# Laying a small first piece on 30 partitions instead of 120, and declaring implied waits away

## Chip, cores, metric

One core of one Trainium2 chip. The metric is the device time of one execution in microseconds (us), as the median of several; the kernel before takes 394.75 us (394.6 to 394.81, 6 runs). All runs quoted here are fast (none lies over 1.5% above the fastest of its kernel). Ratios are the mean time of one kernel's fast runs over that of the other's of the same rounds, so not quite the ratio of the medians that are quoted beside them.

## The reference

```python
batch, channels, length = 32, 256, 4096      # x: float32, 134.2 MB
p, kernel_size = 2.0, 4
window = np.abs(x[:, :, start:end]) ** p     # start = 4 * i, end = start + 4
result[:, :, i] = (np.mean(window, axis=-1)) ** (1.0 / p)   # 33.6 MB
```

Four neighbours are squared, averaged, and the root is taken: 134 MB in, 34 MB out, and very little arithmetic.

## The kernel before

The data is seen as one flat array. Most of it goes through three big x tiles (128 partitions x 13184 columns), loaded on the SyncE queue. ScalarE squares in place, VectorE sums groups of four into an o tile, ScalarE takes the root, and one store per group goes out on ScalarE's queue, the last four on SyncE's. What does not fit these sizes, 840 columns of 128 rows (430 KB), is a small piece of its own, handled first.

```python
    W, O_W = 13184, 6592
    X_SLOTS, O_SLOTS = 3, 2
    ODD = 840
    groups = [2] * 9 + [3, 1]
    late = {7, 8, 9, 10}                       # groups stored on SyncE's queue, at the end
    # ...
    def root(g, o, ends):
        nc.scalar.activation(out=o, in_=o, func=Act.Sqrt, scale=1.0 / k)
        if ends and g not in late:
            store(g, nc.scalar)
    # ...
    Q = 120
    odd = ODD * P // Q                         # 896 columns of 120 rows
    t = o_tiles[1][0:Q, 0:odd]
    nc.sync.dma_start(out=t, in_=xf[(total - ODD) * P:total * P].rearrange("(p w) -> p w", p=Q))
    ahead = 0
    while ahead < n and loads[ahead][0] < X_SLOTS:
        load(ahead)                            # three big loads queued behind it
        ahead += 1
    nc.scalar.activation(out=t, in_=t, func=Act.Square)
    o = o_tiles[1][0:Q, odd:odd + odd // k]
    nc.vector.tensor_reduce(out=o, in_=t.rearrange("p (n j) -> p n j", j=k), ...)
    nc.scalar.activation(out=o, in_=o, func=Act.Sqrt, scale=1.0 / k)
    nc.scalar.dma_start(out=of[...].rearrange("(p w) -> p w", p=Q), in_=o)
    pending = []
    done = 0
    for i in range(n):
        # load ahead; per chunk: Square, total_sum; then the root of the chunk before
        # ...
    for job in pending:
        root(*job[1:])
    for g in sorted(late):
        store(g, nc.sync)
```

Of the kernel before, what the change touches and what calls it, by code (L numbers as in the profile page):

```python
# [1 line left out]

# [4 lines left out]


@with_exitstack
def kernel(  # L10
    ctx: ExitStack,
    tc: tile.TileContext,
    x: bass.AP,
    p: float,
    kernel_size: int,
    out: bass.AP,
):








    nc = tc.nc

    assert float(p) == 2.0, "kernel specialized for p == 2"
    k = int(kernel_size)
    assert k == 4, "kernel specialized for kernel_size == 4"  # L30

    P = nc.NUM_PARTITIONS
    fp32 = mybir.dt.float32
    Act = mybir.ActivationFunctionType
    xf = x.rearrange("b c l -> (b c l)")
    of = out.rearrange("b c l -> (b c l)")
    total = xf.shape[0] // P

    W, O_W = 13184, 6592
    X_SLOTS, O_SLOTS = 3, 2  # L40
    slots = [[(W, [4416, 4384, 4384])]] * 18
    slots += [[(6592, [3296, 3296])] * 2, [(6592, [3296, 3296]), (4216, [2112, 2104])]]
    ODD = 840
    groups = [2] * 9 + [3, 1]
    late = {7, 8, 9, 10}
    in_x = {9: (2, 0), 10: (2, 4944)}
    FINE, ENDS, LAG = range(22), (), 1
    PAIRS = 16


    loads = [(s, sum(w for w, _ in slot[:j]), *slot[j]) for s, slot in enumerate(slots)
             for j in range(len(slot))]
    n = len(loads)
    assert sum(w for _, _, w, _ in loads) + ODD == total

    firsts = [sum(groups[:g]) for g in range(len(groups))]
    assert sum(groups) == n
    group_of = [g for g, count in enumerate(groups) for _ in range(count)]
    columns = [sum(w for _, _, w, _ in loads[firsts[g]:firsts[g] + groups[g]])
               for g in range(len(groups))]  # L60

    x_pool = ctx.enter_context(tc.tile_pool(name="x_pool", bufs=1))
    o_pool = ctx.enter_context(tc.tile_pool(name="o_pool", bufs=1))

    x_tiles = [x_pool.tile([P, W], fp32, name=f"xt{j}") for j in range(X_SLOTS)]
    o_tiles = [o_pool.tile([P, O_W], fp32, name=f"ot{j}") for j in range(O_SLOTS)]
    ctx.enter_context(tc.manual_schedule())

    def block(flat, g, div):
        at, width = sum(columns[:g]) * P // div, columns[g] * P // div  # L70
        return flat[at:at + width].rearrange("(p w) -> p w", p=P)

    xs = {}

    def load(i):
        s, at, w, _ = loads[i]
        v = x_tiles[s % X_SLOTS][:, at:at + w]
        g = group_of[i]
        src = sum(loads[j][2] for j in range(firsts[g], i))
        nc.sync.dma_start(out=v, in_=block(xf, g, 1)[:, src:src + w])  # L80
        xs[i] = v

    ots = {}

    def store(g, queue):
        queue.dma_start(out=block(of, g, k), in_=ots[g])  # L86

    def root(g, o, ends):
        nc.scalar.activation(out=o, in_=o, func=Act.Sqrt, scale=1.0 / k)  # L89
        if ends and g not in late:  # L90
            store(g, nc.scalar)

    def total_sum(o, v, i):
        add = mybir.AluOpType.add
        if i < PAIRS:
            nc.vector.tensor_reduce(  # L96
                out=o, in_=v.rearrange("p (n j) -> p n j", j=k),
                axis=mybir.AxisListType.X, op=add,
            )
            return  # L100

        q = v.rearrange("p (n j) -> p n j", j=k)
        front = v[:, 0:v.shape[1] // 2]
        h = front.rearrange("p (n j) -> p n j", j=2)
        nc.vector.tensor_tensor(out=h, in0=q[:, :, 0:2], in1=q[:, :, 2:4], op=add)  # L105
        nc.vector.tensor_tensor(out=o, in0=h[:, :, 0], in1=h[:, :, 1], op=add)  # L106


    Q = 120
    odd = ODD * P // Q  # L110
    t = o_tiles[1][0:Q, 0:odd]
    nc.sync.dma_start(out=t, in_=xf[(total - ODD) * P:total * P].rearrange("(p w) -> p w", p=Q))  # L112
    ahead = 0
    while ahead < n and loads[ahead][0] < X_SLOTS:
        load(ahead)
# [3 lines that stand above are left out]
    nc.vector.tensor_reduce(  # L119
        out=o, in_=t.rearrange("p (n j) -> p n j", j=k),  # L120
        axis=mybir.AxisListType.X, op=mybir.AluOpType.add,
    )
    nc.scalar.activation(out=o, in_=o, func=Act.Sqrt, scale=1.0 / k)  # L123
    nc.scalar.dma_start(
        out=of[(total - ODD) * P // k:total * P // k].rearrange("(p w) -> p w", p=Q), in_=o,
    )
    pending = []
    done = 0
    for i in range(n):
        s, _, w, chunks = loads[i]  # L130
        while ahead < n and loads[ahead][0] < s + X_SLOTS:
            load(ahead)
            ahead += 1
        g = group_of[i]
        if i == firsts[g]:
            t, first = (o_tiles[g % O_SLOTS], 0) if g not in in_x else (x_tiles[in_x[g][0]], in_x[g][1])
            ots[g] = t[:, first:first + columns[g] // k]
            summed = rooted = 0
        assert sum(chunks) == w
        c = 0  # L140
        for step in chunks:
            v = xs[i][:, c:c + step]
            nc.scalar.activation(out=v, in_=v, func=Act.Square)  # L143
            total_sum(ots[g][:, summed:summed + step // k], v, i)
            while pending and pending[0][0] <= done - LAG:
                root(*pending.pop(0)[1:])
            done += 1
            c += step
            summed += step // k
            ends = summed == columns[g] // k  # L150
            if ends or i in FINE or (i in ENDS and c == w):
                pending.append((done - 1, g, ots[g][:, rooted:summed], ends))
                rooted = summed
# [6 lines that stand above are left out]
# [1 line left out]
_INS = ['x', 'p', 'kernel_size']  # L161
_OUTS = [((32, 256, 1024), 'float32')]

_NUMBERS = {'p': 2.0, 'kernel_size': 4}


# [26 lines left out]
```

## Time and profile before

| | before |
|---|---|
| time, median | 394.75 us |
| profiled span | 392.8 us |
| VectorE / ScalarE busy | 69% / 74% |
| the two transfer queues, share of 16 engines | 85.2% + 14.0% |
| bytes moved, mean rate | 167.79 MB, 427 GB/s |

The prediction below shows the lines behind this table. One more view is the chain of waits by line; each share is the part of the span in which the chain ran through that line:

```profile
by line: DMA xt<-in_x_dram 62.4%; ACT xt L143 17.0%; DVE ot L96 8.4%; issue 3.6%; ACT ot L89 3.3%; ACT xt L89 1.2%; DVE xt L105 0.8%; DVE xt L106 0.4%; ACTq L86 0.3%; SPq L80 0.2%; SPq L112 0.1%; ACTq L89 0.0%
```

Loads of x lead. "issue" at 3.6%, 14 us, is time for which the chain saw no releaser; whether it could be saved by removing waits is one of the questions here.

### The profile page before, as it was taken

To read this page: it belongs to the slowest core of one execution; us is meant where nothing else is said; L and a number is where in the kernel's file an instruction comes from. 1 tells how busy PE (TensorE), PEld (TensorE's weight loads), DVE (VectorE), ACT (ScalarE), POOL (GpSimd) and SP (SyncE) were. 2 spreads that over 40 slices of the span, in tenths; PEclk is the share of its full clock that TensorE was granted. 3 is DMA by queue.
4 is the path that set the end of the run, shared out by engine and by line. 5 is a ranking of instruction groups with operands and counts; after the bars stand their busy time and mean duration, and the time that the engine had idled before them with its cause. 6 is when DMAs were issued, how large, how long until landed. Compare 5 with 4: busy or idle time off the path is not lost.

```text
span 392.8 us, 341 instructions
## 1 busy us (share of the span) xinstructions
DVE 271.8 (69%) x77; ACT 292.5 (74%) x128; POOL 0.2 (0%) x4
## 2 busy tenths in 40 slices
DVE  1059989594959495949594959495949494778781
ACT  3088987776776777677867786868586859899990
POOL 0000000000000000000000000000000000000000
DMA  9999999999999989999999999999999999999997
GB/s 361 420 429 446 446 446 384 430 470 430 389 432 473 430 387 435 467 430 422 432 435 430 427 435 427 430 435 459 459 404 430 459 438 430 395 430 432 429 432 315
DMA packets 5024, 167.79 MB, mean 427 GB/s; under 512 B 558, under 2 KB 678, under 8 KB 926
## 3 DMA queue, kind: packets, MB, share of 16 engines
q1 hardware_dynamic: 3879, 144.04, 85.2%
q10 hardware_dynamic: 1143, 23.73, 14.0%
q14 instruction: 2, 0.02, 0.0%
HBM read 134.22 MB, written 33.55 MB: 427 GB/s over the span
## 4 chain that ended last, share of the span: by engine, by line
DMA 62%; ACT 21%; DVE 10%; issue 4%; SPq 0%; ACTq 0%
DMA xt<-in_x_dram 62%; ACT xt L143 17%; DVE ot L96 8%; ACT ot L89 3%; ACT xt L89 1%; DVE xt L105 1%; DVE xt L106 0%; ACTq L86 0%; SPq L80 0%; SPq L112 0%; ACTq L89 0%
## 5 line engine op out<-in xcount | busy, mean ns | idle before, releaser
L143 ACT ACTIVATE xt<-xt 128x4384 f32<-128x4384 f32 (+4 forms) x62 | 229.6, 3705 | 85.1 <-DMA xt<-in_x_dram 81.9
L96 DVE TENSOR_REDUCE ot<-xt 128x1096 f32<-128x4384 f32 (+1 forms) x48 | 227.0, 4731 | 90.1 <-ACT xt L143 89.8
L89 ACT ACTIVATE ot<-ot 128x1096 f32<-128x1096 f32 (+1 forms) x54 | 59.8, 1107 | 1.8 <-DVE ot L96 1.1
L105 DVE TENSOR_TENSOR xt<-xt 128x1648 f32<-128x1648 f32 (+4 forms) x14 | 28.4, 2032 | 16.0 <-ACT xt L143 16.0
L89 ACT ACTIVATE xt<-xt 128x824 f32<-128x824 f32 (+2 forms) x8 | 6.5, 817 | 1.9 <-DVE xt L106 1.9
L106 DVE TENSOR_TENSOR ot<-xt 128x1096 f32<-128x1096 f32 (+1 forms) x6 | 7.8, 1303 | 0.2
L106 DVE TENSOR_TENSOR xt<-xt 128x824 f32<-128x824 f32 (+2 forms) x8 | 7.5, 939 | 0.3
L119 DVE TENSOR_REDUCE ot<-ot 120x224 f32<-120x896 f32 x1 | 1.1, 1086 | 5.7 <-ACT ot L117 5.7
L117 ACT ACTIVATE ot<-ot 120x896 f32<-120x896 f32 x1 | 0.9, 949 | 2.7 <-DMA ot<-in_x_dram 2.7
L117 ACT ACT_TABLE_LOAD x1 | 1.3, 1283 | 0.7 <-PEq L174 0.7
L123 ACT ACT_TABLE_LOAD x1 | 1.3, 1283 | 0.0
L123 ACT ACTIVATE ot<-ot 120x224 f32<-120x224 f32 x1 | 0.4, 389 | 0.0
L174 POOL MEMSET const-bfloat16-1.0<- 128x1 bf16 x1 | 0.1, 101 | 0.0
L174 POOL MEMSET const-uint8-127<- 128x1 uint8 x1 | 0.1, 101 | 0.0
L174 POOL MEMSET const-float32-0.0<- 128x1 f32 x1 | 0.1, 99 | 0.2 <-issue 0.2
L174 POOL MEMSET const-float32-1.0<- 128x1 f32 x1 | 0.1, 99 | 0.0
## 6 DMA issues: line engine op xcount, KB each, us to landing
xt<-in_x_dram SPq DMA_DIRECT2D x18, 6592.0 KB, 39.9
out_dram<-ot ACTq DMA_DIRECT2D x7, 3296.0 KB, 27.6
xt<-in_x_dram SPq DMA_DIRECT2D x3, 3296.0 KB, 29.4
out_dram<-ot SPq DMA_DIRECT2D x2, 3296.0 KB, 30.0
out_dram<-xt SPq DMA_DIRECT2D x1, 2472.0 KB, 10.4
xt<-in_x_dram SPq DMA_DIRECT2D x1, 2108.0 KB, 26.8
out_dram<-xt SPq DMA_DIRECT2D x1, 527.0 KB, 7.1
ot<-in_x_dram SPq DMA_DIRECT2D x1, 420.0 KB, 4.0
```

The source lines that it names most:

```text
L89: nc.scalar.activation(out=o, in_=o, func=Act.Sqrt, scale=1.0 / k)
L96: nc.vector.tensor_reduce(out=o, in_=v.rearrange("p (n j) -> p n j", j=k), axis=mybir.AxisListType.X, op=add,)
L105: nc.vector.tensor_tensor(out=h, in0=q[:, :, 0:2], in1=q[:, :, 2:4], op=add)
L106: nc.vector.tensor_tensor(out=o, in0=h[:, :, 0], in1=h[:, :, 1], op=add)
L117: nc.scalar.activation(out=t, in_=t, func=Act.Square)
L119: nc.vector.tensor_reduce(out=o, in_=t.rearrange("p (n j) -> p n j", j=k), axis=mybir.AxisListType.X, op=mybir.AluOpType.add,)
L123: nc.scalar.activation(out=o, in_=o, func=Act.Sqrt, scale=1.0 / k)
L143: nc.scalar.activation(out=v, in_=v, func=Act.Square)
L174: nc = _bacc.Bacc("TRN2", target_bir_lowering=False, num_devices=1)
```

## The change

The small piece gets two descriptors for each of 15 DMA engines instead of eight (a descriptor moves one row of a transfer, and the trace records each as one packet), and waits that, in the words of the code, follow from other waits are declared away. The diff, cut to its core (a list `by_act` of ScalarE's instructions, `sums` of VectorE's and `stores` of the stores are kept for it; `by_load` stays empty):

```diff
+    def follows(ins, before):
+        for b in before:
+            tc.declare_no_dep(ins.ins, b.ins, reason="follows from other waits")
     def root(g, o, ends):
-        nc.scalar.activation(out=o, in_=o, func=Act.Sqrt, scale=1.0 / k)
+        r = nc.scalar.activation(out=o, in_=o, func=Act.Sqrt, scale=1.0 / k)
+        follows(r, by_act[:-1] + list(stores.values()))
+        by_act.append(r)
     # total_sum: the same with follows(r, sums[:-1]) on each sum
-    Q = 120
+    Q = 30
     # main loop:
-            nc.scalar.activation(out=v, in_=v, func=Act.Square)
+            r = nc.scalar.activation(out=v, in_=v, func=Act.Square)
+            follows(r, by_act[:-1])
+            by_act.append(r)
```

## The prediction

> **What bounds the kernel now.** I read the page's shares first, then its slices and DMA lines, then the timeline of the two ends, because a kernel whose transfers never pause can only be shortened at its ends or by moving fewer or better packets.
>
> The page (engines, then the DMA row of the 40 slices, packets and queues):
> ```profile
> DVE 271.8 (69%) x77; ACT 292.5 (74%) x128; POOL 0.2 (0%) x4
> ...
> DMA  9999999999999989999999999999999999999997
> ...
> DMA packets 5024, 167.79 MB, mean 427 GB/s; under 512 B 558, under 2 KB 678, under 8 KB 926
> ## 3 DMA queue, kind: packets, MB, share of 16 engines
> q1 hardware_dynamic: 3879, 144.04, 85.2%
> q10 hardware_dynamic: 1143, 23.73, 14.0%
> ```
> No compute engine is above 74%, while the two transfer queues together fill 85.2 + 14.0 = 99.2% of 16 engines' span, and the row of slices has no hole before the last. The chain of waits puts most of its time (62.4%) on loads of the x tiles. So the bytes bound the kernel.
>
> Could the end still be a compute tail? ScalarE is 90% busy or more in the last slices. The stretches at the end (length, busy us with counts, clock, DMA share, GB/s) answer that:
> ```profile
> 360.00:376.00 16.00, 12.39 (x9) 16.00 (x9) 0.00 (x0) 1.00 1.00 427
> 376.00:386.00 10.00, 6.73 (x6) 6.84 (x7) 0.00 (x0) 1.00 0.99 425
> 386.00:393.00 7.00, 0.00 (x0) 0.00 (x0) 0.00 (x0) 1.00 0.62 261
> ```
> The last store is issued at 384.8 us (timeline of the SyncE queue, which ends with two stores from 380.26 on, 4.88 us in all), the engines run full until past 386, and still move 7 x 261 = 1.83 MB after 386. From 384.8 on that is 1.83 + 1.2 x 425/1000 = 2.3 MB, some 5.4 us of work at 427 GB/s, already queued or just issued; only 0.54 MB of it is the last store. ScalarE and VectorE could be some 3 to 4 us later in the tail without moving the end. The tail is bound by the queue of stores too.
>
> Last, the start, where the change acts (timeline: start, length, engine, line, operation, idle before and releaser):
> ```profile
> 0.73 0.46 SPq L112 DMA_DIRECT2D ot<-in_x_dram  x1
> 1.24 1.30 SPq L80 DMA_DIRECT2D xt<-in_x_dram  x3
> 4.74 0.95 ACT L117 ACTIVATE ot<-ot 120x896 f32<-120x896 f32 x1 [2.73 <-DMA ot<-in_x_dram]
> 5.71 1.28 ACT L123 ACT_TABLE_LOAD   x1
> 5.72 1.09 DVE L119 TENSOR_REDUCE ot<-ot 120x224 f32<-120x896 f32 x1 [5.72 <-ACT ot L117]
> 7.00 0.39 ACT L123 ACTIVATE ot<-ot 120x224 f32<-120x224 f32 x1
> 7.42 0.64 ACTq L124 DMA_DIRECT2D out_dram<-ot  x1
> 20.36 7.63 ACT L143 ACTIVATE xt<-xt 128x4416 f32<-128x4416 f32 x2 [12.97 <-DMA xt<-in_x_dram]
> ```
> The odd piece is done with compute at 7.4 us, and both engines then idle until the first big load lands at 20.36: 12.97 us of slack for it.
>
> I also read the trace's single DMA packets, one line of the tile each. They are very regular. A 52736 B row takes 1947 ns, a 26368 B one 978, the 896 B rows of the small store 41, the undisturbed 3584 B rows of the small load 140. The first packet starts at 1.75 us, the last ends at 391.42. All packet times add up to 389.72 us per engine; 1.75 + 389.72 = 391.47, so the engines have practically no idle time between, and 392.8 - 391.4 = 1.4 us of closing work follows. The time is therefore: start of the first packet + packet time of the slowest engine + 1.4, and on top the 1.9 us by which the measured 394.73 exceeds the profiled span, which the change does not touch.
>
> **What the Trainium skill says.** "DMA: Bandwidth & Descriptors", section "Where 436 GB/s comes from", gives 435.2 GB/s for the 16 ports. The trace agrees in size: 52736 B in 1947 ns is 27.1 GB/s per engine, 433 for 16, and the mean over the span is 427. The same page, "Why small descriptors are slow (HBM only)", names a fixed cost of about 3 cycles per packet. Here it is larger: taking 27.2 GB/s off each size leaves 1947 - 1939 = 8 ns, 978 - 969 = 9, 41 - 33 = 8, 140 - 132 = 8, some 7 cycles of its 850 MHz; the measurement decides. The same page, "Queues, rings and completion order", says that an engine goes round the queue rows packet by packet. The trace agrees: the 896 B packets of the small store come about 1.95 us apart on an engine, one after each 1947 ns row of x, which is why 105 KB take 20.7 us to land:
> ```profile
> ot<-in_x_dram SPq DMA_DIRECT2D x1, 420.0 KB, 4.0
> out_dram<-ot ACTq DMA_DIRECT2D x1, 105.0 KB, 20.7
> ```
> "SBUF — State Buffer", "Door 1: The DMA port swizzle", puts partitions 0 to 31 on 8 of the 16 ports. No run yet shows what that does here, but it is the one risk, below.
>
> **The change part by part.**
>
> *Descriptors.* The small load has 120 rows of 3584 B, the small store 120 of 896 B; afterwards both have 30, of 14336 and 3584 B. The bytes stay. That is 180 packets of 5024 fewer, 12 on each of 15 engines. At 8 ns each: 12 x 8 = 0.10 us off those engines. Checked by rows: load 8 x 140 = 1.12 against 2 x (14336/27.2 + 8 = 535) = 1.07; store 8 x 41 = 0.33 against 2 x 140 = 0.28. Sum -0.10 us, on the path, since the engines never idle. The sixteenth engine gains nothing, but it carries 35.8 KB less and is not last.
>
> *Contention at the start.* The 120 rows took 205 ns in the mean, not 140: 8 x 65 = 0.5 us of crowding per engine, and the first row of x on each engine took 2.15 to 2.54 us in place of 1.95, 0.35 more in the mean. First rows of x ended between 5.5 and 6.1 us. Crowding is thus already paid, some 0.85 us. Afterwards, 430 KB go to 8 ports: 430 KB / (8 x 27.2) = 1.98 us at best against 430 / (15 x 27.2) = 1.05. From 1.75 + some 0.2 for the first access the small load ends at about 3.9, the first row of x, then uncrowded, at 3.9 + 1.95 = 5.9. That lies inside the 5.5 to 6.1 of before. I choose +0.05 for this term, with -0.3 to +0.5 as likely.
>
> *Compute of the odd piece.* The rows get four times as long on a quarter of the lanes. Square: from the groups 128x3296 (2934 ns) and 128x4384 (3843 ns), 0.84 ns an element and 0.18 us fixed, so 3584 elements take 3.2 us, not 0.95. Reduction: 1086 ns at 896 elements and 4719 at 4384 give 1.04 per element, so 3.9, not 1.09. Root: some 0.93, not 0.39. Together 8.0 in place of 2.4, and the small store is issued at about 13 us instead of 7.4. All of that is inside the idle 12.97 us, so 0 on the path. With 2 packets an engine in place of 8, the store should land 6 to 8 us after issue, at about 20 in place of 28; the next writer of that tile comes at 55.5 us, so again 0. For the same reason the wait for this store moves from the first to the second sum of group 1 on VectorE without costing anything.
>
> *Waits.* The comparison of the instruction streams shows no change of order. ScalarE loses eight waits for stores and six waits for its own earlier instructions; VectorE loses one on itself. The store waits had been met before: VectorE had waited for the same store before writing what ScalarE then reads. The self-waits cost nothing visible: at 350.18 the square that carries one starts 0.09 us before the root ahead of it has ended (349.16 + 1.11), and the square at 76.03, with no such wait, also starts 0.09 before its root's end (75.02 + 1.10). Even 14 x 20 ns would vanish in ScalarE's idle time. 0 on the path.
>
> Sum: -0.10 + 0.05 + 0 + 0 = -0.05, say 394.73 - 0.1 = 394.6 after leaving the small chance that the start gets tidier.
>
> **The rivals.** First, the port jam: if the rows are dealt to engines in turn (engine e gets rows e and e+15), the first 15 rows lie on 4 ports, the next 15 on about 4 others, and the load needs 2 x 4 x 527 ns = 4.2 us instead of 2.1. Every engine would be some 2 us behind for good: 396.8. For it: the first rows on the 15 engines took from 138 to 668 ns, as if up to four shared something. Against: later rows ran at 140, with no sharing, and fair sharing should have stretched them all. I give a noticeable delay (over 0.7 us) one chance in seven. Second, the waits matter: a shorter ScalarE tail issues the last stores earlier. Against: 2.3 MB lie ahead of the engines when the last store is issued; even 1 us earlier would leave the end where it is. 394.7. Third, the small descriptors cost more than their own time, because each of the 8 store packets breaks into the stream of loads. Against: x rows beside them took 1947 ns, as elsewhere. If it were true, 0.3 us less: 394.3. Fourth, the slower odd piece delays something. It has 12.97 us of slack and needs 5.6: 394.7.
>
> **Range and chances.** The three runs before lie 0.2 us apart. The terms give -0.4 to +0.5, and the jam a tail to +2. So 394.6, with 394.0 to 395.6 for 8 in 10. A change of 2% would be 7.9 us; nothing in the sum reaches that in either direction: faster 0.005, same 0.985, slower 0.01.
>
> **What would show it.** Right: packets 4844 (5024 - 180), under 2 KB as many as under 512 B, under 8 KB 716; queue shares still 99%; small store issued near 13 us, landed within 8; first square of x between 20.1 and 20.9; the 14336 B packets taking near 1 us each instead of 535 ns, if 8 ports bind. Wrong: a first square later than 21.5 (the jam), the 14336 B packets at 535 (no port limit, then up to 0.5 us gained), holes in the DMA row, or an end that moved with the same start (then the waits or something later did it).

## The result and the profile after

394.65 us median (394.57 to 394.96, 6 runs) against 394.75 (394.6 to 394.81, 6 runs) before. The ratio is 0.9999, with a 95% interval of 0.9986 to 1.0012: the same. The interval is about half a microsecond wide to each side, so a gain of 0.1 us, as forecast, can't be told from none.

The page of the kernel after (engines, packets, queues):

```profile
DVE 274.6 (70%) x77; ACT 295.3 (75%) x128; POOL 0.2 (0%) x4
...
DMA packets 4844, 167.79 MB, mean 427 GB/s; under 512 B 558, under 2 KB 558, under 8 KB 716
...
q1 hardware_dynamic: 3789, 144.04, 85.2%
q10 hardware_dynamic: 1053, 23.73, 14.0%
```

180 packets are gone, exactly as counted; the bytes, the rate and the share of both queues have not moved. Both compute engines work 2.8 us more, for the longer rows of the small piece. Where those lie is in the timeline of its start:

```profile
0.73 0.45 SPq L131 DMA_DIRECT2D ot<-in_x_dram  x1
1.24 1.30 SPq L81 DMA_DIRECT2D xt<-in_x_dram  x3
4.75 3.19 ACT L136 ACTIVATE ot<-ot 30x3584 f32<-30x3584 f32 x1 [2.74 <-DMA ot<-in_x_dram]
7.96 1.28 ACT L142 ACT_TABLE_LOAD   x1
7.97 3.87 DVE L138 TENSOR_REDUCE ot<-ot 30x896 f32<-30x3584 f32 x1 [7.97 <-ACT ot L136]
11.88 0.95 ACT L142 ACTIVATE ot<-ot 30x896 f32<-30x896 f32 x1 [2.64 <-DVE ot L138]
12.86 0.63 ACTq L143 DMA_DIRECT2D out_dram<-ot  x1
20.48 7.63 ACT L162 ACTIVATE xt<-xt 128x4416 f32<-128x4416 f32 x2 [7.66 <-DMA xt<-in_x_dram]
```

The small store is issued at 12.86 us instead of 7.42, but ScalarE still waits for the first big load, 7.66 us instead of 12.97. The first square starts at 20.48 instead of 20.36. The list of transfers shows the one large local gain:

```profile
ot<-in_x_dram SPq DMA_DIRECT2D x1, 420.0 KB, 4.0
out_dram<-ot ACTq DMA_DIRECT2D x1, 105.0 KB, 7.8
```

The small store lands 7.8 us after its issue instead of 20.7, because an engine passes one packet of it between two rows of x, and there are now two in place of eight. Nobody was waiting for it. The end, in the same stretches as before:

```profile
376.00:386.00 10.00, 6.73 (x6) 6.86 (x7) 0.00 (x0) 1.00 0.98 424
386.00:393.00 7.00, 0.00 (x0) 0.00 (x0) 0.00 (x0) 1.00 0.63 266
```

Within two per cent the same end. Last, the chain of waits by line:

```profile
by line: DMA xt<-in_x_dram 62.5%; ACT xt L162 20.4%; DVE ot L110 8.4%; ACT ot L101 3.2%; ACT xt L101 1.2%; DVE xt L121 0.8%; DVE xt L123 0.4%; ACTq L98 0.3%; issue 0.3%; SPq L81 0.2%; SPq L131 0.1%
```

This looks like a success, and is not one: "issue" fell from 3.6% to 0.3%, 13 us, with the time unchanged. The squares' share rose by 3.4%. With the extra wait gone, the profile's bookkeeping follows the chain through the square instead of losing it: at 57 us the chain before has 3.72 us of "issue", the chain after a square of 3.86 us. A share of the chain is a label on time, not time that can be had.

### The profile page after: what moved, and what is told of

Same layout as the page of the kernel before. It is cut to its first block, busy times and chain, and to the rows that moved or that the text cites. A ratio compares the mean times of both kernels' runs of the same rounds, so it can differ in the third digit from the quotient of the medians.

```text
span 392.9 us, 329 instructions
## 1 busy us (share of the span) xinstructions
DVE 274.6 (70%) x77; ACT 295.3 (75%) x128; POOL 0.2 (0%) x4
## 2 busy tenths in 40 slices
DMA packets 4844, 167.79 MB, mean 427 GB/s; under 512 B 558, under 2 KB 558, under 8 KB 716
## 4 chain that ended last, share of the span: by engine, by line
DMA 63%; ACT 25%; DVE 10%; SPq 0%; ACTq 0%; issue 0%
DMA xt<-in_x_dram 63%; ACT xt L162 20%; DVE ot L110 8%; ACT ot L101 3%; ACT xt L101 1%; DVE xt L121 1%; DVE xt L123 0%; ACTq L98 0%; SPq L81 0%; SPq L131 0%
## 5 line engine op out<-in xcount | busy, mean ns | idle before, releaser
L138 DVE TENSOR_REDUCE ot<-ot 30x896 f32<-30x3584 f32 x1 | 3.9, 3874 | 8.0 <-ACT ot L136 8.0
L136 ACT ACTIVATE ot<-ot 30x3584 f32<-30x3584 f32 x1 | 3.2, 3189 | 2.7 <-DMA ot<-in_x_dram 2.7
L142 ACT ACTIVATE ot<-ot 30x896 f32<-30x896 f32 x1 | 0.9, 948 | 2.6 <-DVE ot L138 2.6
```

## The experiments

Ten kernels ran, all correct. The single packets quoted are from the records of the trace, a row of a tile each. These records do not name the engine, so a figure "per engine" is a sum over all packets divided by 16.

**1. Only the layout** (`Q = 30` in the kernel before).

> Only the rows are changed (30 instead of 120), no wait is taken away. Theory (the transfers are the bound and never pause; the change has two small terms of opposite sign in the start): the same time as the changed kernel, ratio to before 0.9985 to 1.001; mean packet time of the small load near 850 ns as in the changed kernel; first square of x near 20.5 us. Rival 'small packets break the stream of loads': 0.3 us or more faster than before, ratio 0.999 or less, and the gain is here, not in the other half of the change.

394.69 us (394.52 to 394.70, 5 runs) against 394.70 (394.57 to 395.08, 9 runs); ratio 0.9997, interval 0.9984 to 1.0009. The same, as the theory said. The small load's rows took 922 ns in the mean, and the first square started at 20.64 us. The stated rival, small packets breaking the stream of loads, is not seen: a gain of 0.3 us should have shown in the medians, which are 0.01 apart, though the interval alone would not exclude it. The trace of the kernel before speaks against it as well: the 120 packets of the small store pass between 11.3 and 25.7 us, and none of the 176 rows of x that start between 7 and 28 us took longer than 1956 ns, against the usual 1947.

**2. Only the waits** (the changed kernel with `Q = 120`).

> Only the waits are declared away, the rows stay 120. Theory: no change, ratio 0.9990 to 1.0010, 15 instructions or so fewer in the trace, same starts in the tail within 0.1 us. Rival 'the waits cost something': 0.2 us or more faster, with the last store issued earlier than 384.8 us and the end following it.

394.61 us (394.60 to 394.80, 5 runs) against 394.70; ratio 0.9997, interval 0.9984 to 1.0010. Again the same. The trace has 330 instructions, 11 fewer than before (not the 15 expected), though the waits in it are 15 fewer, as the prediction lists them. The two last stores begin at 380.19 us instead of 380.26; the squares that lost a self-wait start as before, for instance at 350.16 here and 350.18 there. The chain's "issue" share already falls to 0.2% here, so nearly all of it belongs to the waits and was worth nothing. (It is 2.7% in experiment 1, where no wait was declared away: the label moves by itself too.)

**3. The small piece on all 128 rows.**

```diff
-    Q = 120
+    Q = 128
```

> The small piece on 128 rows, 8 on each of 16 engines, no wait taken away. Theory (the crowding at the start comes from small rows and rows of x of different engines writing to the same group of partitions; with 128 rows both are dealt out alike): packets of the small load near their undisturbed 132 ns in the mean (not 205), first rows of x near 1950 ns (not 2300), first square of x some 0.6 us earlier (19.6 to 20.0), time 0.4 to 0.9 us less, ratio 0.9977 to 0.9990. Rival (the crowding is the first access of many engines at once, whatever the rows): packets stay near 200 ns, time within 0.2 us of before.

394.92 us (394.34 to 395.08, 5 runs); ratio 1.0001, interval 0.9988 to 1.0015. My expectation of a gain failed. Half of its premise held: later rows of the small load did run at 132 ns, and the small load landed in 3.2 us instead of 4.0. But the first rows still took up to 613 ns, the mean was 178, and the first rows of x took 2115 ns in the mean, not 1950. The first square, in the timeline, is only 0.3 us earlier:

```profile
20.04 7.63 ACT L143 ACTIVATE xt<-xt 128x4416 f32<-128x4416 f32 x2 [13.48 <-DMA xt<-in_x_dram]
```

And even this did not arrive at the end: around 58 us a set of rows of x was slow by 0.75 us per engine in sum, against 0.43 in the kernel before. Experiment 10 asks what that is.

**4. No small piece at all**: its columns go into the last load.

```diff
-    ODD = 840
+    ODD = 0
-    ... (4216, [2112, 2104])]]
+    ... (5056, [2528, 2528])]]
     # and the block from Q = 120 to the small store is removed
```

> No separate small piece: its 840 columns are put into the last load. Same bytes, right result. Theory: the first x row starts at 1.75 to 2.4 us, not 2.9 to 3.9; 240 packets fewer and no crowding, so 0.5 to 0.9 us less, ratio 0.9977 to 0.9988. The compute tail grows by some 1.4 us (last store issued near 386 us), which the queue of stores should hide. Rival (the small piece is free, it fills time in which the load of x could not yet start): the bytes come back at the end and the time is the same or up to 1 us more.

394.69 us (394.52 to 394.95, 5 runs); ratio 0.9998, interval 0.9985 to 1.0011. The gain that I had expected did not come. The first square does start 0.9 us earlier:

```profile
19.45 7.63 ACT L129 ACTIVATE xt<-xt 128x4416 f32<-128x4416 f32 x2 [17.45 <-DMA xt<-in_x_dram]
```

and the columns come back in the last load and the last stores: in the stretch after 386 us, where only stores are left, this kernel moves 282 GB/s and the kernel before 261. So the rival named beforehand is right: the piece as such is about free, its bytes cost the same wherever they lie. (The last store was issued no later, since the whole chain had begun earlier.) The packets show why the start could not gain more. With no small rows to crowd them, the 16 first rows of x took 2266 to 3208 ns, 2717 in the mean, where a later row takes 1947. So rows are slow in the first microseconds after the start even where no small rows are met. How much is lost does depend on the layout: above undisturbed packet times, the first 7 us cost an engine 0.88 us in the kernel before, 0.78 here and 0.56 with 128 rows. Why the start is slow is not shown.

**5. More packets: each load as two halves.**

```diff
-        nc.sync.dma_start(out=v, in_=block(xf, g, 1)[:, src:src + w])
+        half = w // 2
+        whole = block(xf, g, 1)
+        nc.sync.dma_start(out=v[:, :half], in_=whole[:, src:src + half])
+        nc.sync.dma_start(out=v[:, half:], in_=whole[:, src + half:src + w])
```

> The kernel before with every load issued as two halves of its columns: same bytes, 2816 more packets of rows and 352 more of 4 bytes. It enlarges the term that the change shrinks (packets of an engine) without touching the start's small piece. Theory (each packet costs its engine some 8 ns more than its bytes, and the engines never pause): 176 x 8 + 22 x 9 = 1.6 us more per engine, all on the path: 396.2 to 396.5, ratio 1.0035 to 1.005. Rival (packet cost hides behind other transfers, or the DMA engines are not the bound): within 0.3 us of before.

396.39 us (396.14 to 396.67, 4 runs) against 394.69; ratio 1.0039, interval 1.0024 to 1.0054. 1.70 us more, where 1.6 was worked out. The packets, in the page of this kernel:

```profile
DMA packets 8193, 167.80 MB, mean 425 GB/s; under 512 B 910, under 2 KB 1030, under 8 KB 1278
```

A term too small to see in the change is visible when it is made sixteen times as large: some 8 ns per packet, on the path, the same for rows of 26 KB. The packet records of this kernel give the term by itself: every packet at its usual time adds up to 389.94 us per engine, against 388.18 in the kernel before, 1.76 us more. By the same figure the change's 12 packets fewer per engine are worth 0.1 us.

**6 and 7. A later tail.** `C` needless instructions stand before the last root, on a tile that is no longer used, C = 1 and 2.

```diff
-    for job in pending:
+    for job in pending[:-1]:
         root(*job[1:])
+    for _ in range(C):
+        nc.scalar.activation(out=x_tiles[0][:, 0:4384], in_=x_tiles[0][:, 0:4384], func=Act.Sqrt)
+    root(*pending[-1][1:])
```

> One square-sized instruction (3.84 us, of which 1.53 fit into ScalarE's wait before the last root) is put before the last root, so the last store is issued some 2.3 us later, near 387.1. Theory (the stores ahead of it keep the engines full until past 389): the end moves by 0 to 0.4 us. Rival (the tail's compute sets the end, so taking waits out of it could have paid): 2.3 us later, 397.0.

394.72 us (394.64 to 394.81, 4 runs) against 394.69; ratio 0.9999, interval 0.9985 to 1.0012. The last pair of stores, in SyncE's timeline, shows that the store was indeed late (380.37 + 6.99, against 380.26 + 4.88). The kernel before, then this one:

```profile
380.26 4.88 SPq L86 DMA_DIRECT2D out_dram<-xt  x2
```

```profile
380.37 6.99 SPq L86 DMA_DIRECT2D out_dram<-xt  x2
```

The stretch after 386 us of the same kernel:

```profile
386.00:393.00 7.00, 0.00 (x0) 1.00 (x2) 0.00 (x0) 1.00 0.63 266
```

The engines did not notice: the kernel before moved 261 GB/s there.

> Two such instructions: the last store is issued some 6.1 us later, near 390.9. Now the queue of stores should have run dry, so the slack is measured: theory 2.5 to 4 us later than before (396.9 to 399). Rival (slack over 6 us): no change. Rival (no slack): 6.1 us later, 400.8.

396.65 us (396.54 to 397.56, 4 runs); ratio 1.0047, interval 1.0031 to 1.0062. Now the queue runs dry before the last store comes, in the stretches of this kernel:

```profile
386.00:390.00 4.00, 0.00 (x0) 3.97 (x2) 0.00 (x0) 1.00 0.79 341
390.00:392.00 2.00, 0.00 (x0) 2.00 (x2) 0.00 (x0) 1.00 0.02 10
392.00:395.80 3.80, 0.00 (x0) 0.09 (x1) 0.00 (x0) 1.00 0.36 142
```

Some 6.1 us of delay cost 1.96 us, by the medians, so the slack of the tail is about 4.1 us, a little more than the 3 to 4 of the prediction. My expectation here, a loss of 2.5 to 4 us, was missed. The profiled run of this kernel was itself 1.3 us behind before the tail, so the slack is taken from the times.

**8. A much slower start.** Twenty-four needless instructions on ScalarE after the small piece.

```diff
+    for _ in range(24):
+        nc.scalar.activation(out=t, in_=t, func=Act.Sqrt)
     pending = []
```

> The compute of the small piece is followed by 24 needless instructions on ScalarE, some 23 us, so ScalarE reaches the first big square near 30 us instead of 20.4: ten times the slowing by the new layout, and 10 us beyond ScalarE's idle time. Theory (three loads are queued ahead, the next is needed only when load 2 lands near 51 us, and it is issued at 38.7 now): the fourth load is issued up to 10 us later, just in time or up to 1 us late, and the end moves by 0 to 1.5 us. Rival (work in the start is on the path once the idle time is used up): 10 us later.

396.32 us (396.02 to 396.64, 4 runs) against 394.69; ratio 1.0039, interval 1.0026 to 1.0053. 1.63 us more, just over the stated 1.5, and far from the rival's 10. The first square starts at 31.5 us, 11.1 us late; the fourth big load is issued at 49.83 instead of 38.71, and the third one is through at about 51. The first square and the issue of the fourth load in the timeline of this kernel, then the stretches around it:

```profile
31.50 7.61 ACT L145 ACTIVATE xt<-xt 128x4416 f32<-128x4416 f32 x2
49.83 14.80 SPq L80 DMA_DIRECT2D xt<-in_x_dram  x2
```

```profile
46.00:50.00 4.00, 3.94 (x2) 3.99 (x3) 0.00 (x0) 1.00 0.98 422
50.00:54.00 4.00, 4.00 (x1) 4.00 (x2) 0.00 (x0) 1.00 0.96 356
54.00:58.00 4.00, 3.88 (x2) 4.00 (x3) 0.00 (x0) 1.00 1.01 435
```

A dip to 356 GB/s, four microseconds long: (422 - 356) / 422 x 4 = 0.6 us lost there. At 51.0 us only 8 of the 16 engines had a packet under way; the idle time of all of them makes 0.5 us per engine. Engines that had fallen idle then began rows that took up to 3225 ns, as at the start of the kernel. These slow rows, and a larger set at 67 to 72 us, cost 1.1 us per engine more than the slow rows of the kernel before in the same part of the trace, so with the idle time nearly all of the 1.63 us is accounted for. The changed kernel's compute, 5.4 us longer, is hidden twice: by ScalarE's 7.66 us of remaining idle time, and behind that by some 10 us until the next load is needed.

**9. Sixty-four rows**: all 16 engines, but, by the port map of "SBUF — State Buffer" that the prediction cites, still only the 8 ports (groups of partitions) that 30 rows use.

```diff
-    Q = 120
+    Q = 64
```

> The small piece on 64 rows of 6720 B: all 16 engines, 4 rows each, and again only the 8 groups of partitions that the 30 rows use. An undisturbed row would take 6720/27.2 + 8 = 255 ns. Theory (the 8 groups limit the small load to 430 KB in 2 us): rows take near 500 ns in the mean, also the later ones, the small load's last row ends near 3.9 us. Rival (there is no such limit; only the first accesses after a start are slow, as the run with 128 rows suggests): the first row of each engine takes up to 0.8 us, the later ones 255. Time within 0.4 us of before either way.

394.89 us (394.78 to 395.01, 4 runs) against 394.68; ratio 1.0005, interval 0.9987 to 1.0023. Rows took 441 ns in the mean, between the two theories; some later rows ran at 255, others at 300 to 520. Spreading each row's bytes evenly over its time gives the rate of the small load in steps of a quarter microsecond:

| kernel | rows | highest rates of the small load, GB/s | its last row ends |
|---|---|---|---|
| before | 120 | 310, 359 | 3.90 us |
| 128 rows | 128 | 379, 371 | 3.59 us |
| after | 30 | 292, 285 | 3.81 us |
| only the layout | 30 | 245, 242 | 3.95 us |
| 64 rows | 64 | 296, 296 | 4.33 us |

The 64 rows started at 2.05 us, 0.3 us later than all the others, so their 4.33 compares with 4.03. At their highest rates the layouts with fewer groups of partitions stay below the others (other profiles with 120 rows reach some 310 to 370), but not at a clean 218 (8 x 27.2). Over its whole length, from first start to last end, the small load hardly differs: 200 GB/s before, 208 after, 194 with only the layout and 188 with 64 rows; only the 128 rows stand out with 235. A limit of that kind, softer than forecast, would fit the highest rates, but it is not shown. I can't separate it from the slowness of the start: the load is over in 2 us.

**10. An earlier first big store.**

```diff
-    groups = [2] * 9 + [3, 1]
-    late = {7, 8, 9, 10}
-    in_x = {9: (2, 0), 10: (2, 4944)}
+    groups = [1, 1] + [2] * 8 + [3, 1]
+    late = {8, 9, 10, 11}
+    in_x = {10: (2, 0), 11: (2, 4944)}
```

> The first group of outputs is cut in two, so the first big store is issued near 40 us, not 56.5; the rest is as before. It asks what the slow rows at 58 to 62 us are (30 rows of x, 0.42 us an engine in the kernel before, 0.76 in the run with 128 rows, which seem to give back what the start gained). Theory (they belong to the first big store): they move to some 2 us after the new first store and are gone at 58 to 62. Rival (they belong to that load, or to that time): they stay. Time within 0.4 us of before.

394.89 us (394.62 to 394.94, 4 runs) against 394.68; ratio 1.0004, interval 0.9988 to 1.0020. The first two big stores, in ScalarE's timeline of this kernel:

```profile
41.03 0.37 ACTq L86 DMA_DIRECT2D out_dram<-ot  x1
59.41 0.34 ACTq L86 DMA_DIRECT2D out_dram<-ot  x1
```

The set at 58 to 62 us is gone, and a new one comes with the earlier store, so it goes with the first big store and not with that time. But it did not simply move along: 11 rows from 42.6 us on, some 2 us after the store's issue, lost only 0.1 us per engine, and the larger part, 16 rows at once and 0.55 us per engine, came at 50.3 to 51.0, 9 us after the issue (in the kernel before all lay within 5.5 us). The edit also changes the order in which the first loads read x, which was not tested alone. No such set came with the later stores; later on no more than three rows at a time stand out in these kernels. In the slowed start of experiment 8, whose first big store was issued at 65.45 us, a set lies at 67 to 72, but there the fifth load began late at the same time, so it decides nothing.

The sum of the set per engine varies from one profile to the next (before 0.43 us, after 0.31, only the layout 0.09, only the waits 0.44, 128 rows 0.75, 64 rows 0.06, no piece 0.96). It is smallest where the first 7 us lost most (only the layout 1.22 us per engine, 64 rows 1.19) and largest where they lost least (no piece 0.78, 128 rows 0.56). But the kernels of experiments 6 and 7, whose instructions up to the tail are those of the kernel before, have 0.50 and 0.77: chance alone makes some 0.3 us. Why the first store does this is open, and so is whether the 0.3 us that the 128 rows won at the start are given back there by necessity or by chance.

No version beats the two kernels: apart from the three that cost 1.6 to 2 us (experiments 5, 7 and 8), all medians lie between 394.6 and 394.9 us.

## Why the prediction was right

- **The bound.** Confirmed. 16 engines that never pause set the time: more packets went straight into it (1.70 us for a worked-out 1.6), and 2.3 us more compute in the tail or 5.4 us more in the start did not.
- **Packets.** 4844, with 558 under 2 KB and 716 under 8 KB, as listed. The forecast gain of 0.10 us is too small to see in the times; experiment 5 supports its price per packet, and the packets at their usual times add up to 388.09 us per engine, against 388.18 before.
- **Contention at the start.** The size was within the stated -0.3 to +0.5 but chosen too low, and part of the reason was wrong. The choice was +0.05 us. The last of the 16 first rows of x ended at 6.07 us before and after, but at 6.22 with the same 30 rows in experiment 1, and the first square came 0.12 and 0.28 us later than before. Above undisturbed packet times, the first 7 us cost 0.88 us per engine before (0.84 to 0.96 in five other profiles with 120 rows), 1.07 after and 1.22 in experiment 1, so the term is nearer to +0.2 or +0.3. That the time shows none of it is in part luck: beside the 0.09 us of fewer packets, the slow rows at the first big store happened to cost 0.1 and 0.3 us less in these two profiles. "The first row of x, then uncrowded" was a wrong step: it took 2387 ns in the mean after the change (2328 before), not 1950. Experiment 4 shows such slowness without any small piece. The rows of 14336 B took 852 ns in the mean, between the 535 of no limit and the near 1 us of the full one, so that step of the forecast was too sharp as well. (The 0.35 us by which the first rows of x were slow before is 0.38 in the records, and the sum of -0.05 was taken as -0.1; neither matters here.)
- **Compute of the piece.** Square 3.19, sum 3.87, root 0.95 us, against 3.2, 3.9 and 0.93; the store at 12.86 (about 13), landed after 7.8 (6 to 8). All hidden.
- **Waits.** Worth nothing that these times can show (0.09 us between the medians of experiment 2, which has them alone); experiments 6 and 7 give the reason: about 4 us of slack in the tail.
- **The rivals.** The port jam (+2 us) did not occur: the small load ended at 3.81 us, no later than before. Small packets breaking the stream: not seen in experiment 1, and no row of x beside them was slow. The slower piece delays nothing: 7.66 us of idle time were left.

What remains uncertain is the sign of the last 0.1 us, which these times cannot give.

## What to carry to other kernels

Before tidying waits or descriptors, ask whether the engines that move the bytes ever pause; if they don't, as here, look first at packets, bytes and the two ends, and price each from the packet records. A term too small to measure is best tested by making it many times larger, and slack by adding delay until the end moves. A share of the chain of waits that shrinks is no gain until the time shrinks too.

## What the Trainium skill lacked or had wrong

- "DMA: Bandwidth & Descriptors", section "Why small descriptors are slow (HBM only)", gives some 3 cycles per packet on an internal bus, and 32 bytes of metadata beside it. All that a packet costs above its bytes is here 8 to 9 ns at every size from 840 B to 52736 B, some 7 cycles if they are of the page's 850 MHz, and the split loads confirm it on the path (+1.70 us for 198 packets more per engine, of which 22 are of 4 bytes). Another section of that page, "Measured (HBM→SBUF, 128 partitions, SWDGE, issued from GpSimd)", has about 10.5 ns per packet for the smallest transfers, which is nearer.
- The same page, section "Queues, rings and completion order", has packets of typically 9 to 17 descriptors between two changes of queue. Here an engine changed after every single row, as the prediction took it: the eight 896 B rows of the small store came about 2 us apart, not together.
- No page that I read has the slowness of rows in the first microseconds after the engines start together: 2717 ns in the mean and up to 3208 for a row that later takes 1947, and up to 3225 when they restart after a short pause.
- No page that I read has the slow rows at the first big store, 0.06 to 0.96 us per engine, which lay at 58 to 62 us and, with an earlier store, at 42.6 to 51.
- "SBUF — State Buffer", section "Door 1: The DMA port swizzle", gives about 218 GB/s for partitions 0 to 31, which lie on 8 ports. The small load showed 242 to 296 at its highest quarter microseconds on 30 and 64 rows, against 310 to 379 on 120 and 128, but over its whole length 188 to 208 against 200 and 235: neither a limit nor its size is settled by so short a transfer.
